# A transformer block on one core: the order of the first feed-forward product on three engines, written out by hand

## The chip, the cores and the metric

The kernel runs on one core of one Trainium2 chip. The metric is the device time of one execution in microseconds (us), from the first to the last instruction with what lies around them; the time of a kernel is the median of its runs.

## What is computed

One block of a hybrid encoder on 512 tokens of width 2048: an input projection, two kinds of attention, an output projection, and a feed-forward part of width 8192. The change touches the first of the two feed-forward products:

```python
h2 = rmsnorm(x, g_mlp[l])
u = jax.nn.relu(jnp.einsum('bsd,df->bsf', h2, w_up[l]))      # the first product
x = x + jnp.einsum('bsf,fd->bsd', u * u, w_down[l])          # the second
return rmsnorm(x, g_final)
```

## The kernel before

Everything is float32 in and out. The matrix engine works in a faster form of float32 with fewer bits, so an operand is split into a high part (a cast on ACT, `split`, line 65) and a low part (the difference, on DVE, line 66), and a product is the sum of high times high and the two cross products.

**The first feed-forward product** is cut into `NU` = 32 units of 256 columns of `w_up`. In each unit the product is a 2 by 2 block product with seven instead of eight multiplications (Winograd's form of Strassen's scheme). The seven are numbered 1 to 7. The activations' seven forms, `F[p]` (high and low, tiles `fh` and `fl`), are made once. The weights of a unit are made into seven parts: blocks 1, 2 and 3 are plain blocks of `w_up`; 5, 6 and 7 are differences of blocks, and 4 is a difference of block 2 and part 6. For most units ("early" ones) the differences for 5, 6 and 7 were made during the attention stage and lie in DRAM (`td`); the others load plain blocks and make them on DVE in the stage itself (`self.raw`, lines 898, 899 and 901).

A unit (`class Unit`) loads three tiles from the pool `rw` of five buffers: `r` (block 1 and part 6), `q` (parts 5 and 7) and a wide one (blocks 2 and 3). `split_part` makes high and low part of one of the seven; `hi_lo` hands out four sets of buffers in turn (three named `wh`/`wl`, one `wx`). `multiply` issues 8 matmuls with the high part over 512 columns (both activation halves, line 920) and 8 with the low part over 256 (line 922). Products 1, 6, 7 and 4 go into one PSUM bank (A, `psa`) and add up there; 2 goes into B, 5 and then 3 into C. Between them `close` takes sums out: after 1, 6 and 7 ACT copies A into a tile `s` (line 933), so the next product into A has to wait for that copy. DVE then adds B or C and writes a quarter of the result `c` (lines 940 to 952). The copies after 1 and 7 share one buffer, so that one must be used up before the next is made. After product 3 the quarter is complete, and ACT applies relu and square (lines 954 and 955).

Two units make a pair, whose result `c` is the input of the second product. It needs seven forms of it in turn, again split into high and low (`store_form`, `hidden_form`): ACT casts into a tile `st` (three buffers), DVE makes the low part in the same tile, and SP stores it to DRAM (`ufd`, line 962).

**What sets the order.** The loop over units (line 1149 on) calls products in the order new 1, old 4, new 5, new 6, old 3, new 2, new 7, with one form stored behind four of them. In this loop no engine's order is written by hand: the framework's scheduler sorts all engines' instructions by its own timing model. Each engine then runs its list strictly in that order, and so does SP, which issues all the DMAs.

Of the kernel before, what the change touches and what calls it, by code (L numbers as in the profile page):

```python
# [40 lines left out]
def block_kernel(ctx, tc, x, g_attn, w_in, b_f, g_out_sb, g_out_fox, w_out, g_mlp, w_up, w_down, g_final, y):  # L41
# [21 lines left out]
    def split(hi, lo, src, scale=None):  # L63
        if scale is None:
            ins = casts[0] = act.copy(hi, src)  # L65
            lows[0] = dve.tensor_tensor(lo, src, hi.bitcast(F32), op=ALU.subtract)  # L66
# [780 lines left out]
    class Unit:  # L847
        def __init__(self, u):
            self.u = u
            first, last = (up_rows[i][:, :, 2 * u * P:2 * (u + 1) * P] for i in range(2))  # L850
# [6 lines left out]
            def blocks():  # L857
                return rw.tile([P, 2, KC // 2, P], F32, tag="rw", name="wu")

            def wide(src):  # L860
                raw = rw.tile([P, KC // 2, 2 * P], F32, tag="rw", name="wu")
                sp.dma_start(raw, src)
                return [raw[:, :, j * P:(j + 1) * P] for j in range(2)]

            r, q = blocks(), blocks()
            b11, t2, t1, t3 = r[:, 0], r[:, 1], q[:, 0], q[:, 1]
            sp.dma_start(b11, first[:, :, :P])
            self.raw = u not in early
            if self.raw:
                sp.dma_start(t1, first[:, :, P:])  # L870
                sp.dma_start(t3, last[:, :, P:])
                sp.dma_start(t2, last[:, :, P:])
            else:
                for t_, j in ((t1, 0), (t2, 2), (t3, 1)):
                    sp.dma_start(t_, td[u][:, j])
            b21, b22 = wide(last)
            self.b = {1: b11, 5: t1, 6: t2, 2: b21, 7: t3, 3: b22, 4: b21}
            self.open_banks()

        def open_banks(self):  # L880
            self.B, self.C, self.A = (ups.tile([P, NT], F32, tag=c, name=f"ps{c}") for c in "bca")
# [11 lines left out]
            self.b.update({3: b22, 4: b21})  # L893

        def split_part(self, p):
            hi, lo = (w.rearrange("p (a b) -> p a b", b=P) for w in hi_lo(2 * NT))
            if p == 5 and self.raw:
                dve.tensor_tensor(self.b[7], self.b[7], self.b[5], op=ALU.subtract)
                dve.tensor_tensor(self.b[5], self.b[5], self.b[1], op=ALU.subtract)
            if p == 6 and self.raw:  # L900
                dve.tensor_tensor(self.b[6], self.b[6], self.b[5], op=ALU.subtract)
            if p == 4 and self.u < 2:
                dve.tensor_tensor(self.b[4], self.b[4], self.b[6], op=ALU.subtract)
            split(hi, lo, self.b[p])
            if p == 2 and self.u > 1:
                dve.tensor_tensor(self.b[4], self.b[4], self.b[6], op=ALU.subtract)
            self.parts[p] = hi, lo

        def product(self, p):
            if p not in self.parts:  # L910
                self.split_part(p)
            self.multiply(p)
            self.close(p)

        def multiply(self, p):
# [5 lines left out]
            for a in range(KC // 2):  # L921
                pe.matmul(ps[:, :2 * P], lo[:, a, :], F[p][a // 4][:, a % 4, 0, :], start=False, stop=a == KC // 2 - 1, skip_group_check=True)  # L922

        def close(self, p):
# [5 lines left out]
            t1, t2 = slice(0, 2 * P), slice(2 * P, NT)  # L930
            if p in (1, 6, 7):
                self.m = (sr if p == 6 else sm).tile([P, NT], F32, tag="m", name=f"s{p}", bufs=2 if p == 6 else 1)
                act.copy(self.m, self.A)
                if p == 6:
                    self.m6 = self.m
                if p == 1:
                    self.m1 = self.m

            def sums(out, m):
                dve.tensor_tensor(out, m[:, t1], m[:, t2], op=ALU.add)  # L940

            if p == 7:
                dve.tensor_tensor(self.m, self.m, self.C, op=ALU.add)
                sums(self.c[:, 1, t2], self.m)
            if p == 2:
                dve.tensor_tensor(self.m1, self.m1, self.B, op=ALU.add)
                sums(self.c[:, 0, t1], self.m1)
            if p == 4:
                act.copy(self.c[:, 0, t2], self.A[:, t1])
                dve.tensor_tensor(self.c[:, 0, t2], self.c[:, 0, t2], self.A[:, t2], op=ALU.add)  # L950
            if p == 3:
                dve.tensor_tensor(self.m6, self.m6, self.C, op=ALU.add)
                sums(self.c[:, 1, t1], self.m6)
                act.activation(self.c, self.c, AF.Relu)
                act.activation(self.c, self.c, AF.Square)

    def store_form(p, c, u):
        st = wp.tile([P, 2, 2, 2 * P], F32R, tag="wraw", name="st")
        hidden_form(p, c, (st[:, 0], st[:, 1]), c[:, :, 1, 2 * P:])
        (g0, j0), (g1, j1) = (at_unit[u + i] for i in range(2))  # L960
        if g0 == g1:
            sp.dma_start(ufd[g0][p][:, :, j0:j0 + 2, :], st.bitcast(F32))
# [185 lines left out]
    old = u1  # L1148
    for u in range(2, NU + 1):
        new = Unit(u) if u < NU else None  # L1150
        if u == NU - 1:
            for p in ORDER:
                load_uf(p, GROUPS[0])
            b_first = load_b(GROUPS[0], 0)
        if new is None:
            second(1, b_first, 0, GROUPS[0][1], True)
        for i, (who, p) in enumerate(((new, 1), (old, 4), (new, 5), (new, 6), (old, 3), (new, 2), (new, 7))):
            if who is None:
                continue
# [1 line left out]
            if u == 3 and p == 6:
                v2 = cp.tile([P, TB], F32, name="v2")
                dve.tensor_reduce(v2, ss2, axis=mybir.AxisListType.X, op=ALU.add)
                dve.tensor_scalar(v2, v2, 1.0 / D, EPS, op0=ALU.mult, op1=ALU.add)
                ev = cp.tile([P, TB], F32, name="ev")
                dve.scalar_tensor_tensor(ev, v2, EPS, v2, op0=ALU.mult, op1=ALU.mult)
            if todo and u < NU - 1 and i in (0, 2, 4, 5):
                store_form(*todo.pop(0))
            if p == 3 and who.u % 2 == 1 and who.u < NU - 2:
                todo += [(q, who.pair, who.u - 1) for q in A_ORDER]  # L1170
# [161 lines left out]
```

## Time and profile before

| | |
|---|---|
| median of 3 runs | 2067.24 us (2059.48 to 2069.8) |
| profiled execution | 2065.28 us, its span 2063.6 us |
| busy PE, DVE, ACT | 99%, 80%, 52% of the span |
| first feed-forward product | about 795 to 1437 us of the span |

PE is the matrix engine, DVE and ACT the two elementwise engines, SP the queue that issues the DMAs. Times in the trace are microseconds from the start of the span. A group's row gives its count, its busy time, the mean of one in ns, and the idle time of its engine just ahead of it with what ended it. A matmul's end in the trace is modelled; its start is measured.

### The profile page before, as it was taken

What the parts mean: (1) busy time and instruction counts of PE and PEld (TensorE: products, weight loads), DVE (VectorE), ACT (ScalarE), POOL (GpSimd) and SP (SyncE); (2) the same over time, 40 slices, a digit from 0 to 9 for tenths busy, and PEclk for the clock granted to TensorE, in tenths of its full rate; (3) what the DMA queues carried; (4) which work ended last, traced back from release to release, by engine and by line L of the source; (5) the groups of instructions that cost most, each with busy time, mean ns of one, the idle gap of its engine ahead of it and who ended that gap; (6) DMA issues with size and microseconds to landing.
All of it is one profiled execution on the core that took longest, in us unless ns stands there. A gap on an engine that the chain in (4) does not pass through costs nothing.

```text
span 2063.6 us, 26764 instructions
## 1 busy us (share of the span) xinstructions
PE 2033.8 (99%) x10188; PEld 1727.3 (84%) x10188; DVE 1656.2 (80%) x1866; ACT 1071.4 (52%) x1419; POOL 59.7 (3%) x73
## 2 busy tenths in 40 slices
PE   8999999999999999999999999999999999999998
PEld 8888888888888888888888888888888888888886
DVE  4767767767777779888888888978889889888886
ACT  5334334444546577656656666655744444443433
POOL 0000000000101000000000000000000000000003
PEclk9999999999999999999999999999999999999999
DMA  7888977888764867777876877777875764764722
GB/s 237 276 289 277 293 256 263 285 268 278 251 200 139 271 226 222 241 258 251 271 240 228 262 246 247 260 249 248 295 247 214 267 243 152 269 234 134 267 91 102
DMA packets 371728, 492.60 MB, mean 239 GB/s; under 512 B 12760, under 2 KB 258568, under 8 KB 362512
## 3 DMA queue, kind: packets, MB, share of 16 engines
q1 hardware_dynamic: 370640, 488.77, 71.5%
q10 hardware_dynamic: 960, 2.13, 0.3%
q8 instruction: 80, 1.31, 0.2%
q14 instruction: 48, 0.39, 0.1%
HBM read 373.39 MB, written 117.46 MB: 238 GB/s over the span
## 4 chain that ended last, share of the span: by engine, by line
PE 91%; DMA 3%; DVE 3%; ACT 2%; issue 1%; SPq 0%; ACTq 0%; DVEq 0%
PE psa L920 10%; PE accd L99 8%; PE accd L100 8%; PE accd L98 8%; PE accq L98 5%; PE accq L99 5%; PE accq L100 5%; PE psa L922 5%; PE psc L920 5%; PE psb L920 3%; PE accv L98 3%; PE accv L99 3%; PE accv L100 3%; PE psc L922 2%; DMA ufd<-st 2%; PE psb L922 1%
## 5 line engine op out<-in xcount | busy, mean ns | idle before, releaser
L65 ACT CAST wh<-wraw 128x1024 fp32r<-128x1024 f32 (+2 forms) x157 | 160.9, 1025 | 241.2 <-PE accq L99 117.3
L66 DVE TENSOR_TENSOR wl<-wraw,wh 128x1024 fp32r<-128x1024 f32 (+2 forms) x157 | 186.5, 1189 | 101.6 <-ACT wh L65 101.1
L65 ACT CAST wh<-wd 128x1024 fp32r<-128x1024 f32 (+1 forms) x134 | 132.6, 999 | 182.0 <-PE accd L100 125.5
L65 ACT CAST wh<-wu 128x1024 fp32r<-128x1024 f32 x160 | 166.9, 1049 | 107.3 <-PE psa L920 39.0
L66 DVE TENSOR_TENSOR wl<-wu,wh 128x1024 fp32r<-128x1024 f32 x160 | 194.9, 1222 | 29.5 <-ACT wh L65 23.9
L98 PE MATMUL accq<-hH,wh 128*128 128x512 f32 x512 | 201.2, 393 | 0.0
L100 PE MATMUL accq<-hH,wl 128*128 128x512 f32 x512 | 199.9, 390 | 0.0
L99 PE MATMUL accq<-hL,wh 128*128 128x512 f32 x512 | 199.7, 390 | 0.0
L66 DVE TENSOR_TENSOR wl<-wd,wh 128x1024 fp32r<-128x1024 f32 (+1 forms) x134 | 153.3, 1155 | 34.2 <-ACT wh L65 34.0
L99 PE MATMUL accd<-wl,uf 128*128 128x512 f32 x428 | 166.8, 390 | 0.4 <-DVE wl L66 0.4
L98 PE MATMUL accd<-wh,uf 128*128 128x512 f32 x428 | 166.6, 390 | 0.1
L100 PE MATMUL accd<-wh,uf 128*128 128x512 f32 x428 | 166.6, 389 | 0.0
L65 ACT CAST wx<-wd 128x1024 fp32r<-128x1024 f32 (+1 forms) x90 | 89.5, 1001 | 118.0 <-PE accd L100 77.4
L66 DVE TENSOR_TENSOR wx<-wd,wx 128x1024 fp32r<-128x1024 f32 (+1 forms) x90 | 103.3, 1158 | 21.9 <-ACT wx L65 21.8
L99 PE MATMUL accd<-wx,uf 128*128 128x512 f32 x292 | 114.0, 390 | 0.5 <-DVE wx L66 0.3
L98 PE MATMUL accd<-wx,uf 128*128 128x512 f32 x292 | 113.6, 390 | 0.2 <-ACT wx L65 0.2
L100 PE MATMUL accd<-wx,uf 128*128 128x512 f32 x292 | 113.7, 389 | 0.0
L100 PEld LDWEIGHTS accq<-hH,wl 128*128 128x128 f32 x512 | 96.1, 188 | 20.1
L99 PEld LDWEIGHTS accq<-hL,wh 128*128 128x128 f32 x512 | 96.2, 188 | 19.0
L98 PEld LDWEIGHTS accq<-hH,wh 128*128 128x128 f32 x512 | 96.2, 188 | 18.8
L1028 DVE TENSOR_TENSOR m<-m,accd 128x1024 f32<-128x1024 f32 x84 | 102.4, 1219 | 11.4 <-PE accd L100 11.3
L920 PE MATMUL psa<-fh,wh 128*128 128x512 f32 x392 | 106.9, 393 | 0.0
(308 smaller groups left out, 4829.8 us busy)
## 6 DMA issues: line engine op xcount, KB each, us to landing
ufd<-st SPq DMA_DIRECT2D x98, 512.0 KB, 6.1
wd<-in_w_down_dram SPq DMA_DIRECT2D x48, 1024.0 KB, 7.3
wraw<-in_w_in_dram SPq DMA_DIRECT2D x84, 512.0 KB, 5.8
uf<-ufd SPq DMA_DIRECT2D x42, 1024.0 KB, 6.4
wu<-in_w_up_dram SPq DMA_DIRECT2D x66, 512.0 KB, 6.9
wu<-in_w_up_dram SPq DMA_DIRECT2D x32, 1024.0 KB, 8.5
sums<-in_w_up_dram SPq DMA_DIRECT2D x60, 512.0 KB, 5.6
td<-sums SPq DMA_DIRECT2D x20, 1536.0 KB, 5.9
```

The costliest lines, as they stand in the source:

```text
L65: ins = casts[0] = act.copy(hi, src)
L66: lows[0] = dve.tensor_tensor(lo, src, hi.bitcast(F32), op=ALU.subtract)
L98: pe.matmul(out, sh, mh, start=first, stop=False, skip_group_check=True)
L99: pe.matmul(out, sh, ml, start=False, stop=False, skip_group_check=True)
L100: pe.matmul(out, sl, mh, start=False, stop=last, skip_group_check=True)
L920: pe.matmul(ps, hi[:, a, :], both, start=a == 0 and p in (1, 2, 5), stop=False, skip_group_check=True)
L922: pe.matmul(ps[:, :2 * P], lo[:, a, :], F[p][a // 4][:, a % 4, 0, :], start=False, stop=a == KC // 2 - 1, skip_group_check=True)
L1028: dve.tensor_tensor(M[p][:, :, db, :], M[p][:, :, db, :], ps, op=ALU.add)
```

## The change

From unit 2 to unit 30 the loop is replaced by a table `SLOTS` with one list of steps for even and one for odd units, which sets the order on ACT and DVE as written (`tc.manual_schedule` for both) and on PE (its manual order now reaches to the end of this loop). A step names what is done and for which unit: `P` a product, `c` a cast, `l` a low part, `m` ACT's copy of bank A, `a` DVE's additions, `rs` one of the three sums of a unit that makes its own weights, `b4` the difference for product 4, `ld` a load, `sq` relu and square, each for `o` (the old unit), `u` (this one) or `n` (the next); `fs`, `fc`, `fl` and `fd` are sum, cast, low part and store of one of the seven forms of an earlier pair. The sum of a form now stands ahead of its cast as a step of its own and may overwrite a quarter of `c`. The units that make their own weights become 3, 7, 9, 11, 13, 15, 17, 19, 23, 25, 27 and 29; they were 2, 5, 7, 10, 13, 15, 18, 21, 23, 26, 29 and 31 (twelve either way). The number of instructions on each engine and of DMAs stays the same; unit 31 and all that follows are ordered by the scheduler as before.

PE, at the end of unit 29 (`psa_12215`) and the start of unit 30 (`psa_12404`, `psc_12403`), before:

```order
L920 MATMUL psa_12215<-fh7_6265,wh_12370 128x512 x4
L920 MATMUL psa_12215<-fl7_6266,wh_12370 128x512 x4
L922 MATMUL psa_12215<-fh7_6265,wl_12371 128x256 x4
L922 MATMUL psa_12215<-fl7_6266,wl_12371 128x256 x4
L922 MATMUL psa_12404<-fl1_6258,wl_12406 128x256
L922 MATMUL psc_12403<-fh5_6542,wl_12455 128x256 x4
L922 MATMUL psc_12403<-fl5_6543,wl_12455 128x256 x4
L920 MATMUL psa_12215<-fh4_6261,wx_12432 128x512 x4
```

The same place now (unit 29 is `psa_12226`, unit 30 `psa_12416` and `psc_12415`):

```order
L931 MATMUL psa_12226<-fh7_6265,wl_12310 128x256 x4
L931 MATMUL psa_12226<-fl7_6266,wl_12310 128x256 x4
L929 MATMUL psa_12416<-fh1_6257,wh_12333 128x512 x4
L929 MATMUL psa_12416<-fl1_6258,wh_12333 128x512 x4
L931 MATMUL psa_12416<-fh1_6257,wl_12334 128x256 x4
L931 MATMUL psa_12416<-fl1_6258,wl_12334 128x256 x4
L929 MATMUL psc_12415<-fh5_6542,wx_12385 128x512 x4
L929 MATMUL psc_12415<-fl5_6543,wx_12385 128x512 x4
L931 MATMUL psc_12415<-fh5_6542,wx_12386 128x256 x4
L931 MATMUL psc_12415<-fl5_6543,wx_12386 128x256 x4
L929 MATMUL psa_12226<-fh4_6261,wh_12389 128x512 x4
```

Unit 30's products 1 and 5 moved as a whole between unit 29's 7 and 4, where before their low halves were split off and only nine short matmuls stood between.

ACT at the same place, before (`s7_12390` is the copy of unit 29's bank after product 7, `st` a form's cast, L954 and L955 are relu and square of unit 28):

```order
L954 ACTIVATE c_12174<-c_12174 128x1024
L65 CAST st_12474<-c_11805 128x512
L955 ACTIVATE c_12174<-c_12174 128x1024
L65 CAST wh_12501<-wu_12211 128x1024
L65 CAST wh_12553<-wu_12395 128x1024
L933 COPY s7_12390<-psa_12215 128x512
```

Now (the copy is `s7_12433`):

```order
L962 ACTIVATE c_12218<-c_12218 128x1024
L963 ACTIVATE c_12218<-c_12218 128x1024
L938 COPY s7_12433<-psa_12226 128x512
L910 CAST wh_12436<-wu_12248 128x1024
L910 CAST wh_12439<-wu_12133 128x1024
L938 COPY s1_12447<-psa_12416 128x512
L910 CAST wx_12467<-wu_12312 128x1024
L978 CAST st_12474<-c_11846 128x512
L978 CAST st_12476<-c_11846 128x512
```

The copy moved ahead of the casts, and the forms' casts behind it.

DVE, where unit 29 makes its own weights, before (L898, L899 and L901 are the three sums, `wu_12206` and `wu_12205` unit 29's tiles):

```order
L898 TENSOR_TENSOR wu_12206<-wu_12206 128x1024
L940 TENSOR_TENSOR c_11805<-s7_12018 128x256
L906 TENSOR_TENSOR wu_12028<-wu_12028,wu_12022 128x8x128
L899 TENSOR_TENSOR wu_12206<-wu_12206,wu_12205 128x1024
L66 TENSOR_TENSOR wl_12182<-wu_12023,wh_12181 128x1024
L950 TENSOR_TENSOR c_11805<-c_11805,psa_11846 128x256
L901 TENSOR_TENSOR wu_12205<-wu_12205,wu_12206 128x1024
L952 TENSOR_TENSOR s6_11940<-s6_11940,psc_11845 128x512
```

Now (L884 are the sums, `wu_12098` and `wu_12072` unit 29's tiles):

```order
L914 TENSOR_TENSOR wx_12168<-wu_12072,wx_12167 128x1024
L943 TENSOR_TENSOR c_11846<-c_11846,psa_11854 128x256
L884 TENSOR_TENSOR wu_12098<-wu_12098 128x1024
L884 TENSOR_TENSOR wu_12098<-wu_12098,wu_12072 128x1024
L951 TENSOR_TENSOR s6_11970<-s6_11970,psc_11853 128x512
L953 TENSOR_TENSOR c_11846<-s6_11970 128x256
L884 TENSOR_TENSOR wu_12072<-wu_12072,wu_12098 128x1024
L914 TENSOR_TENSOR wl_12195<-wu_12098,wh_12194 128x1024
```

The sums moved behind unit 29's first low part and the addition after unit 27's product 4; two stand in a row, and the addition after product 3 is done before the third.

The core of the diff:

```diff
-    early = [u for u in range(NU) if u % 8 not in (2, 5, 7)]
+    early = [u for u in range(NU) if u % 2 == 0 or u in (1, 5, 21, 31)]
...
+        def raw_sum(self, p):
             if self.raw:
...
+                a, b = {7: (7, 5), 5: (5, 1), 6: (6, 5)}[p]
+                dve.tensor_tensor(self.b[p], self.b[a], self.b[b], op=ALU.subtract)
...
+    class Form:
...
+        def add(self):
+            a, b, op = {5: (self.a21, self.a22, ALU.add), 6: (self.a22, self.a11, ALU.subtract),
+                        7: (self.a11, self.a21, ALU.subtract), 3: (self.a12, self.a22, ALU.subtract)}[self.p]
+            dve.tensor_tensor(self.src, a, b, op=op)
+
+        def high(self):
+            self.st = wp.tile([P, 2, 2, 2 * P], F32R, tag="wraw", name="st")
+            act.copy(self.st[:, 0], self.src)
...
-    for who, p in ((u0, 6), (u1, 5), (u0, 7), (u1, 6), (u0, 4), (u1, 7), (u0, 3)):
+    SLOTS = [("P u 1; m o 7; fs 6; c u 6; c o 3; a o 7; ld n r; m u 1; P u 5; l u 6; l o 3; c u 2; ld n q; "
...
+             ("P u 1; fc 0; fl 0; fc 1; ld n r; m o 7; c u 6; a o 7; P u 5; c o 3; l u 6; l o 3; fd 0; fl 1; "
...
+    rows_cm = tc.manual_schedule(engines={act.engine, dve.engine})
+    rows_cm.__enter__()
...
+    for u in range(2, NU - 1):
+        units_[u + 1] = Unit(u + 1)
+        at = {"o": units_[u - 1], "u": units_[u], "n": units_[u + 1]}
+        first_of = u - 3 - (u + 1) % 2
+        at["u"].open_banks()
+        for step in SLOTS[u % 2].split(";"):
...
+    rows_cm.__exit__(None, None, None)
     out_cm.__exit__(None, None, None)
...
-        for i, (who, p) in enumerate(((new, 1), (old, 4), (new, 5), (new, 6), (old, 3), (new, 2), (new, 7))):
+        for i, (who, p) in enumerate(((new, 1), (new, 5), (old, 4), (new, 6), (old, 3), (new, 2), (new, 7))):
```

More of the change, by code (lines that the diff above doesn't have):

```diff
@@ L855, in __init__ @@
                 return
[L857 to L867, printed above, removed]
@@ L868, in __init__ @@
-            self.raw = u not in early
-            if self.raw:
[L870 to L878, printed above, removed]
+            self.raw = u not in early
@@ new lines, in __init__, with load_r, load_q @@
+            self.b, self.c = {}, None
+        def load_r(self):
+            self.r = rw.tile([P, 2, KC // 2, P], F32, tag="rw", name="wu")
+            u = self.u
+            sp.dma_start(self.r[:, 0], up_rows[0][:, :, 2 * u * P:(2 * u + 1) * P])
+            sp.dma_start(self.r[:, 1], up_rows[1][:, :, (2 * u + 1) * P:2 * (u + 1) * P] if self.raw else td[u][:, 2])
+            self.b.update({1: self.r[:, 0], 6: self.r[:, 1]})
+        def load_q(self):
+            q = rw.tile([P, 2, KC // 2, P], F32, tag="rw", name="wu")
+            u = self.u
+            for j in range(2):
+                sp.dma_start(q[:, j], up_rows[j][:, :, (2 * u + 1) * P:2 * (u + 1) * P] if self.raw else td[u][:, j])
+            self.b.update({5: q[:, 0], 7: q[:, 1]})
@@ new lines, in load_wide @@
+        def load_wide(self):
+            raw = rw.tile([P, KC // 2, 2 * P], F32, tag="rw", name="wu")
+            u = self.u
+            sp.dma_start(raw, up_rows[1][:, :, 2 * u * P:2 * (u + 1) * P])
+            b21, b22 = (raw[:, :, j * P:(j + 1) * P] for j in range(2))
+            self.b.update({2: b21, 3: b22, 4: b21})
+        def raw_sum(self, p):
+            if self.raw:
+                a, b = {7: (7, 5), 5: (5, 1), 6: (6, 5)}[p]
+                dve.tensor_tensor(self.b[p], self.b[a], self.b[b], op=ALU.subtract)
@@ L895, in split_part, with high, low @@
         def split_part(self, p):
[L896 to L907, printed above, removed]
+            self.high(p)
+            self.low(p)
+        def high(self, p):
+            self.parts[p] = [w.rearrange("p (a b) -> p a b", b=P) for w in hi_lo(2 * NT)]
+            casts[0] = act.copy(self.parts[p][0], self.b[p])
+        def low(self, p):
+            hi, lo = self.parts[p]
+            lows[0] = dve.tensor_tensor(lo, self.b[p], hi.bitcast(F32), op=ALU.subtract)
         def product(self, p):
@@ L913, in product @@
             self.close(p)
+            if p == 3:
+                self.square()
         def multiply(self, p):
@@ L922, in multiply, with copy_sum, add_sum @@
                 pe.matmul(ps[:, :2 * P], lo[:, a, :], F[p][a // 4][:, a % 4, 0, :], start=False, stop=a == KC // 2 - 1, skip_group_check=True)
-        def close(self, p):
+        def copy_sum(self, p):
+            if p == 4:
+                act.copy(self.c[:, 0, 2 * P:], self.A[:, :2 * P])
+                return
+            self.m[p] = (sr if p == 6 else sm).tile([P, NT], F32, tag="m", name=f"s{p}", bufs=2 if p == 6 else 1)
+            act.copy(self.m[p], self.A)
+        def add_sum(self, p):
+            t1, t2 = slice(0, 2 * P), slice(2 * P, NT)
+            if p == 4:
+                dve.tensor_tensor(self.c[:, 0, t2], self.c[:, 0, t2], self.A[:, t2], op=ALU.add)
+                return
             if p == 2:
@@ L929, in close @@
                 self.c = hidden[0][:, self.u % 2]
[L930 to L955, printed above, removed]
+            m = self.m[{7: 7, 2: 1, 3: 6}[p]]
@@ new lines, in add_sum, with close, square @@
+            dve.tensor_tensor(m, m, self.B if p == 2 else self.C, op=ALU.add)
+            out = {7: self.c[:, 1, t2], 2: self.c[:, 0, t1], 3: self.c[:, 1, t1]}[p]
+            dve.tensor_tensor(out, m[:, t1], m[:, t2], op=ALU.add)
+        def close(self, p):
+            if p in (1, 6, 7, 4):
+                self.copy_sum(p)
+            if p in (7, 2, 3, 4):
+                self.add_sum(p)
+        def square(self):
+            act.activation(self.c, self.c, AF.Relu)
+            act.activation(self.c, self.c, AF.Square)
@@ new lines, in block_kernel, with __init__, low, store @@
+    class Form:
+        def __init__(self, i, c, u):
+            self.p, self.u = A_ORDER[i], u
+            self.a11, self.a21, self.a12, self.a22 = (c[:, :, i, j:j + 2 * P] for i in range(2) for j in (0, 2 * P))
+            self.src = {1: self.a11, 2: self.a12, 5: self.a22, 6: self.a22, 4: self.a22, 7: self.a21, 3: self.a12}[self.p]
+        def add(self):
[5 more added lines that the diff above has]
+            act.copy(self.st[:, 0], self.src)
+        def low(self):
+            dve.tensor_tensor(self.st[:, 1], self.src, self.st[:, 0].bitcast(F32), op=ALU.subtract)
+        def store(self):
+            put_form(self.p, self.st, self.u)
@@ L1143, in block_kernel, with store_next @@
     u1.others()
-    for who, p in ((u0, 6), (u1, 5), (u0, 7), (u1, 6), (u0, 4), (u1, 7), (u0, 3)):
-        who.product(p)
-    more_parts.append(parts_hx)
+    def store_next(k=1):
+        for _ in range(k):
+            if todo:
+                store_form(*todo.pop(0))
+    SLOTS = [("P u 1; m o 7; fs 6; c u 6; c o 3; a o 7; ld n r; m u 1; P u 5; l u 6; l o 3; c u 2; ld n q; "
[7 rows of a table added]
+    units_ = {0: u0, 1: u1}
+    units_[2] = Unit(2)
+    u2 = units_[2]
+    for who, p in ((u0, 6), (u1, 5), (u0, 7), (u1, 6)):
+        who.product(p)
@@ new lines, in block_kernel @@
+    u2.load_r()
+    u0.last_sum()
+    u0.product(4)
+    u2.load_q()
+    u2.load_wide()
+    u1.product(7)
+    more_parts.append(parts_hx)
+    rows_cm = tc.manual_schedule(engines={act.engine, dve.engine})
+    rows_cm.__enter__()
+    u0.split_part(3)
+    u2.split_part(1)
+    u2.split_part(5)
+    u1.last_sum()
+    u0.multiply(3)
+    u1.split_part(4)
+    u0.close(3)
+    u0.square()
+    forms = {}
+    for u in range(2, NU - 1):
[4 more added lines that the diff above has]
+        for step in SLOTS[u % 2].split(";"):
+            what, who, *p = step.split()
+            if what[0] == "f":
+                if first_of < 0:
+                    continue
+                i = int(who)
+                if (first_of, i) not in forms:
+                    forms[first_of, i] = Form(i, units_[first_of].pair, first_of)
+                getattr(forms[first_of, i], {"fs": "add", "fc": "high", "fl": "low", "fd": "store"}[what])()
+                continue
+            who, p = at[who], (int(p[0]) if p and p[0].isdigit() else p)
+            if u == 2 and who is u1 and p == 7:
+                continue
+            if what == "ld":
+                getattr(who, {"r": "load_r", "q": "load_q", "w": "load_wide"}[p[0]])()
+            elif what == "b4":
+                who.last_sum()
+            elif what == "sq":
+                who.square()
+            else:
+                getattr(who, {"P": "multiply", "c": "high", "l": "low", "m": "copy_sum", "a": "add_sum", "rs": "raw_sum"}[what])(p)
+        if u == 3:
+            v2 = cp.tile([P, TB], F32, name="v2")
+            dve.tensor_reduce(v2, ss2, axis=mybir.AxisListType.X, op=ALU.add)
+            dve.tensor_scalar(v2, v2, 1.0 / D, EPS, op0=ALU.mult, op1=ALU.add)
+            ev = cp.tile([P, TB], F32, name="ev")
+            dve.scalar_tensor_tensor(ev, v2, EPS, v2, op0=ALU.mult, op1=ALU.mult)
@@ L1147, in block_kernel @@
+    todo += [(q, units_[NU - 4].pair, NU - 4) for q in A_ORDER]
+    rows_cm.__exit__(None, None, None)
     out_cm.__exit__(None, None, None)
-    old = u1
-    for u in range(2, NU + 1):
-        new = Unit(u) if u < NU else None
+    old = units_[NU - 2]
+    for u in range(NU - 1, NU + 1):
+        new = units_.get(u)
         if u == NU - 1:
+            new.open_banks()
             for p in ORDER:
@@ L1154, in block_kernel @@
             b_first = load_b(GROUPS[0], 0)
+            old.close(7)
         if new is None:
             second(1, b_first, 0, GROUPS[0][1], True)
-        for i, (who, p) in enumerate(((new, 1), (old, 4), (new, 5), (new, 6), (old, 3), (new, 2), (new, 7))):
+        for i, (who, p) in enumerate(((new, 1), (new, 5), (old, 4), (new, 6), (old, 3), (new, 2), (new, 7))):
             if who is None:
@@ L1160, in block_kernel @@
             who.product(p)
[L1161 to L1170, printed above, removed]
+            if who is new and p == 2:
+                new.last_sum()
         old = new
```

6 lines of the change are left out of this document (5 added, 1 removed), and 6 rows, old and new, of the table SLOTS.

## The prediction

> **What bounds the kernel now.** I read the page first, then PE's own waits, then the timeline around the longest of them. Two lines: the page's busy row, and the windows row of the first feed-forward product.
>
> ```profile
> PE 2033.8 (99%) x10188; PEld 1727.3 (84%) x10188; DVE 1656.2 (80%) x1866; ACT 1071.4 (52%) x1419; POOL 59.7 (3%) x73
> 830.00:1437.00 607.00, 596.96 (x3396) 524.16 (x3395) 519.81 (x649) 383.45 (x496) 0.00 (x0) 1.00 0.76 250
> ```
>
> PE is the bound; the change adds and removes no matmul. Inside the stage PE is idle for 607.00 - 596.96 = 10.0 us, so this is about the gain on offer. PE's list of waits (us, times, longest) names who ends the idle time:
>
> ```profile
> PE psa L920 <- ACT s L933: 8.5, 7, 2.7
> PE psc L920 <- ACT wh L65: 1.5, 1, 1.5
> ```
>
> The longest of the seven, on three engines' timelines (start, us, what):
>
> ```profile
> 1389.42 1.09 PE L920 MATMUL psa<-fh,wh 128*128 128x512 f32 x4
> 1392.33 0.64 PE L922 MATMUL psc<-fh,wl 128*128 128x256 f32 x4
> 1392.81 0.64 PE L922 MATMUL psc<-fl,wl 128*128 128x256 f32 x4
> 1396.12 1.21 PE L920 MATMUL psa<-fh,wx 128*128 128x512 f32 x4 [2.67 <-ACT s L933]
> 1397.16 1.09 PE L920 MATMUL psa<-fl,wx 128*128 128x512 f32 x4
> ...
> 1387.97 1.05 ACT L954 ACTIVATE c<-c 128x1024 f32<-128x1024 f32 x1
> 1392.12 0.62 ACT L65 CAST st<-c 128x512 fp32r<-128x512 f32 x1 [3.10 <-DMA ufd<-st]
> 1392.65 1.05 ACT L955 ACTIVATE c<-c 128x1024 f32<-128x1024 f32 x1
> 1393.61 1.98 ACT L65 CAST wh<-wu 128x1024 fp32r<-128x1024 f32 x2
> 1395.49 0.57 ACT L933 COPY s<-psa 128x512 f32<-128x512 f32 x1
> ...
> 1383.01 11.00 SPq L962 DMA_DIRECT2D ufd<-st  x4
> ```
>
> Product 7 of the old unit starts at 1389.42 and, at 2.79 us a product (below), ends at 1392.21. Product 4 of that unit accumulates into the same bank and must wait until ACT has copied the bank out. Only nine short matmuls stand between them, 1.08 us. ACT has the copy fifth in its order: it sat 3.10 us before a form's cast, whose tile a store still held, then did a square and two casts for later products. The copy starts at 1395.49 instead of about 1392.5.
>
> **The change part by part.** *The stalls that go.* The waits list gives 8.5 + 1.5 = 10.0 us of idle. By starts each costs more: the last psc group starts at 1392.81, its four take 0.48 (1392.33 to 1392.81 is such a group), so 1396.12 - 1393.29 = 2.83, which is 0.16 over the 2.67 shown; the first group after it takes 1397.16 - 1396.12 = 1.04 against 0.93 in an undisturbed product (below), another 0.11. Eight stalls: 8 x 0.27 = 2.2. After the one at 1073 the granted clock fell:
>
> ```profile
> 1074.40:1078.00 3.60, 3.60 (x15) 3.17 (x14) 1.18 (x3) 1.31 (x2) 0.00 (x0) 0.53 0.99 297
> ```
>
> 3.60 x (1 - 0.53) = 1.7 us. Together 10.0 + 2.2 + 1.7 = 13.9 us, if all go. [...]
>
> *The new order.* PE's rows now run u1, u5, o4, u6, o3, u2, u7 (u this unit, o the one before), each whole. A product's period:
>
> ```profile
> 1012.10 1.09 PE L920 MATMUL psa<-fh,wh 128*128 128x512 f32 x4
> 1013.03 1.07 PE L920 MATMUL psa<-fl,wh 128*128 128x512 f32 x4
> 1013.94 0.64 PE L922 MATMUL psa<-fh,wl 128*128 128x256 f32 x4
> 1014.89 1.09 PE L920 MATMUL psc<-fh,wh 128*128 128x512 f32 x4
> ```
>
> 2.79 us, its low half from 1.84. With u1 at 0 the others start at 2.79, 5.58, 8.37, 11.16, 13.95, 16.74, and the next unit at 19.53. So o4 follows o7 after two products, 5.58 us, not 1.08. Durations for ACT and DVE, groups of the stretch 880 to 1400:
>
> ```profile
> L66 DVE TENSOR_TENSOR wl<-wu,wh 128x1024 fp32r<-128x1024 f32 x136 | 165.6, 1222 | 23.0 <-ACT wh L65 18.1 <-PE psa L922 2.3 <-issue 1.8
> L66 DVE TENSOR_TENSOR st<-c,st 128x512 fp32r<-128x512 f32 x91 | 60.6, 688 | 19.8 <-ACT st L65 19.7
> L940 DVE TENSOR_TENSOR c<-s 128x256 f32<-128x256 f32 x78 | 32.8, 421 | 0.3
> L943 DVE TENSOR_TENSOR s<-s,psc 128x512 f32<-128x512 f32 x26 | 17.7, 683 | 0.8 <-ACT s L933 0.8
> L898 DVE TENSOR_TENSOR wu<-wu 128x1024 f32<-128x1024 f32 x10 | 12.2, 1224 | 7.1 <-DMA wu<-in_w_up_dram 7.1
> L950 DVE TENSOR_TENSOR c<-c,psa 128x256 f32<-128x256 f32 x25 | 10.4, 415 | 0.0
> L65 ACT CAST wh<-wu 128x1024 fp32r<-128x1024 f32 x136 | 141.8, 1049 | 87.8 <-PE psa L920 29.3 <-PE psc L920 16.9 <-DVE wl L66 12.1
> L65 ACT CAST st<-c 128x512 fp32r<-128x512 f32 x91 | 53.5, 619 | 40.2 <-DMA ufd<-st 39.8
> L933 ACT COPY s<-psa 128x512 f32<-128x512 f32 x78 | 45.2, 579 | 11.2 <-DVE c L940 7.9 <-PE psa L922 3.3
> L955 ACT ACTIVATE c<-c 128x1024 f32<-128x1024 f32 x26 | 27.5, 1058 | 0.3
> L949 ACT COPY c<-psa 128x256 f32<-128x256 f32 x26 | 9.7, 371 | 0.7 <-PE psa L922 0.7
> ```
>
> I laid the rows of an even and an odd slot after one another with these, every cast waiting for the high half of the product four before it. ACT's work per pair of units: 14 x 1.05 + 6 x 0.58 + 2 x 0.37 + 4 x 1.06 + 7 x 0.62 = 27.5 us of 39.1. DVE's, with the three raw sums: 14 x 1.22 + 5 x 1.22 + 6 x (0.68 + 0.42) + 2 x 0.42 + 11 x 0.69 = 38.2 of 39.1; without them 34.6. The even slot with raw sums: o7's bank copied by 1.0, DVE's low of u6 done at 3.2 and of o3 at 5.3, the raw sums start at 14.2, o3's addition ends at 17.7, the squares at 20.8, the low of u4 at 22.5. The odd slot starts with DVE 3.0 and ACT 1.3 late: two form casts, o7's copy until 3.2 (o4 needs it by 5.58), u6, o3 and u2 cast by 6.3, u1's bank copied by 6.9 (u6 needs it by 8.37), low of u7 at 13.6 (needed at 18.6), of u4 at 21.3. It returns DVE 1.8 late, and the next even slot ends at 22.5 again. So nothing holds PE, and the tightest places are u1's copy in odd slots (1.4 us) and o7's (2.4 us). The forms' sums ahead of their casts and the weights' sums three rows earlier than their casts cost nothing: they are the same instructions in DVE's slack, which is gone where DVE is over 2.8 us later than this.
>
> *The transfers.* SP's loads keep their places: q behind o3's low, the wide load behind the sum for product 4. What SP is moved past are the stores.
>
> ```profile
> ufd<-st SPq DMA_DIRECT2D x84, 512.0 KB, 5.9
> wu<-in_w_up_dram SPq DMA_DIRECT2D x55, 512.0 KB, 6.7
> DMA to landing us min/median/max: 3.6/6.5/11.0
> DMA to landing us min/median/max: 2.5/5.7/10.7
> ```
>
> (The last two: loads into wu, stores from st.) In an odd slot form 1 is stored at about 8 and form 4's cast at 14.0 needs its tile: at 5.9 us it fits, at 10.7 ACT waits 4.7 us, of which the copy of o7 in the next slot bears 4.2; PE would lose 0.5 + 0.27 = 0.8. In an even slot with raw sums q is issued at 6.1 and 6.5; at 6.7 it lands at 13.2, before 14.2; at 11.0 the sums are 3.3 us late, 2.3 of it borne, and PE loses 1.0 + 0.27 = 1.3. Bounds: 0, and 14 pairs x 0.8 + 12 raw units x 1.3 = 27 us; a gain is excluded, since all of PE's idle time in the stage is already in the 13.9. The medians are the commonest landings, so I take the lower end for both.
>
> *Odd weight sums, the ends.* Twelve units sum their own weights before and after; they now lie in odd units alone, at most one in a pair, as before. The start (units 2 and 3) and the end (unit 31, where the scheduler takes over, and one form of 0.62 + 0.69 us more falls into the second product, beside its work) aren't in the walk. I leave one stall of the mean size there, 10.0 / 8 + 0.27 = 1.5 us; from 0 to 3.
>
> Sum: 13.9 - 1.5 = 12.4 us. The profiled execution's 2065.28 becomes 2052.9. The median of the runs shown, 2067.24, is 1.96 above that execution, so 2054.8.
>
> **The rivals.** *A: the slack isn't there.* Loads and stores land late often enough that PE stalls again, at half the bounds' mean: 7 us of the 13.9 come back. For it: ACT's 39.8 us before form casts, and landings up to 11.0. Against: the waits on raw loads were 7.1 us in seven, and are borne up to 2.3 each. 2067.24 - 13.9 + 1.5 + 7 = 2061.8.
>
> *B, the other side: DVE becomes the bound.* From unit 7 to 19 every odd unit sums its own weights, seven pairs in a row, where before every fourth pair had none. A raw stretch of before:
>
> ```profile
> 1273.00:1313.00 40.00, 39.98 (x231) 35.03 (x229) 35.60 (x45) 26.49 (x36) 0.00 (x0) 1.00 0.77 253
> ```
>
> DVE is busy for about 35.6 us of 39.1, so its order may hold 3.5 us of waits in a pair. In the stage it waited 607.00 - 519.81 = 87.2 us, 5.6 in each of 15.5 pairs. Should a fixed order keep 5.6, a raw pair takes 41.2 and 12 of them cost 25 us, against 13.9 gained: 2067.24 + 11 = 2078. It decides from 3.5 + 13.9 / 12 = 4.7 us a pair. Against it: many of those waits are DVE ahead of its work, and the walk has about 1 us of them.
>
> **How the numbers follow.** 0.5% of 2067.24 is 10.3 us, about what a measurement of this kernel can tell from no change: 2056.9. The forecast (one to three stalls left) has 0.58, A 0.33, B 0.09; so faster 0.58, same 0.33, slower 0.09. The range goes from all 13.9 us gone and half the spread of the three runs (2059.48 to 2069.8, so 5.2) below that, 2048, to A with nearly the whole gain lost, 2066. The forecast's own range is 2050 to 2057.
>
> **What would show it.** Right: PE's waits on ACT's copy of psa under 2 us in total, the window of the stage 12 us shorter at the same PE busy time, product 4 two products behind 7 with no idle, ACT's wait on stores well under 39.8. Wrong: PE waiting for the copy of u1's bank in odd slots, or for a low part; DVE over 37 us busy per pair in units 6 to 19 with PE idle beside it; SP holding stores behind a load. If the stretch behind the stage (1437 to the end) took another time than before, the sum would be wrong at a place that it doesn't look at.

## The result and the profile after

The median went from 2065.11 us (7 runs, 2059.48 to 2069.80) to 2053.72 us (7 runs, 2052.75 to 2056.38). The ratio is 0.9949, its 95% interval 0.9934 to 0.9964: 10.5 us less by the ratio (11.4 by the medians), just over the half per cent that the prediction sets as the bound between faster and the same, with an interval that reaches to both sides of it. The profiled execution took 2052.75 us, the shortest of the seven; its span of 2051.0 us is 12.6 below the one before. Of the four runs of experiment `x2` below, one of 3405.73 us at a granted clock of 0.556 is left out of the median.

The busy row of the page, and the windows row of the part that is ordered by hand (from, to, length, then each engine's busy time, the granted clock, the DMA share, GB/s):

```profile
PE 2029.8 (99%) x10188; PEld 1724.9 (84%) x10188; DVE 1666.0 (81%) x1866; ACT 1077.9 (53%) x1419; POOL 59.7 (3%) x73
830.00:1427.00 597.00, 596.32 (x3409) 524.07 (x3408) 531.20 (x654) 390.93 (x499) 0.00 (x0) 1.00 0.78 253
```

PE is now idle for 597.00 - 596.32 = 0.7 us there, where 10.0 stood before. The stage's length is read from its first matmul to the first one of the second product, on PE's timeline. Before:

```profile
795.28 1.07 PE L920 MATMUL psa<-fh,wh 128*128 128x512 f32 x4
...
1439.73 0.50 PE L98 MATMUL accd<-wx,uf 128*128 128x512 f32 x1 [0.19 <-ACT wx L65]
```

After:

```profile
794.26 1.07 PE L929 MATMUL psa<-fh,wh 128*128 128x512 f32 x4
...
1425.92 0.49 PE L98 MATMUL accd<-wx,uf 128*128 128x512 f32 x1 [0.19 <-ACT wx L65]
```

644.45 us became 631.66, so the stage gave 12.8. It began 1.0 earlier, and what follows it takes 625.1 instead of 623.9, 1.2 longer; 12.8 + 1.0 - 1.2 = 12.6, the whole difference of the spans. The waits of PE in the stage (us, times, longest), all that are left:

```profile
PE psc L929 <- DVE s L951: 0.4, 1, 0.4
PE accd L98 <- ACT wx L65: 0.2, 1, 0.2
```

The seven waits for ACT's copy and the one for a cast are gone; what is left at 830 is a new one, 0.4 us. ACT's own waits on the forms' stores and on the weights' sums, 880 to 1437:

```profile
ACT st L978 <- DMA ufd<-st: 13.4, 11, 1.6
ACT wh L910 <- DVE wu L884: 46.7, 11, 4.3
```

The first fell from 39.8 (longest 6.7); the second is long, and nothing on PE hangs on it. The odd slot, which the prediction called the tightest, on PE and ACT:

```profile
1239.92 1.09 PE L929 MATMUL psa<-fh,wh 128*128 128x512 f32 x4
1242.72 1.09 PE L929 MATMUL psc<-fh,wh 128*128 128x512 f32 x4
1245.51 1.09 PE L929 MATMUL psa<-fh,wx 128*128 128x512 f32 x4
...
1248.30 1.09 PE L929 MATMUL psa<-fh,wh 128*128 128x512 f32 x4
...
1240.72 1.14 ACT L978 CAST st<-c 128x512 fp32r<-128x512 f32 x2
1241.77 0.58 ACT L938 COPY s<-psa 128x512 f32<-128x512 f32 x1
1242.25 1.99 ACT L910 CAST wh<-wu 128x1024 fp32r<-128x1024 f32 x2
1244.76 1.06 ACT L910 CAST wh<-wu 128x1024 fp32r<-128x1024 f32 x1 [0.51 <-PE psc L929]
1245.71 0.58 ACT L938 COPY s<-psa 128x512 f32<-128x512 f32 x1
```

The old unit's product 7 ends at 1239.92, where the new unit's product 1 starts. The copy of its bank ends at 1242.35, so it is 2.43 us late, and product 4 starts at 1245.51, 5.59 after the end of 7. I call the first number the *lateness* and the second, as far as PE's own work fills it, the *distance*; PE stands still where lateness exceeds distance. In even slots the lateness is 0.79. The new unit's product 1 ends at 1242.72, the copy of its bank at 1246.29, and product 6, which needs that bank, starts at 1248.30: 2.0 us to spare. Behind no copy of a bank into `s` is less left in units 4 to 29.

### The profile page after: what moved, and what is told of

It reads as the page before. It is cut to its first block, busy times and chain, and to the rows that moved or that the text cites. A ratio compares the mean times of both kernels' runs of the same rounds, so it can differ in the third digit from the quotient of the medians.

```text
span 2051.0 us, 26668 instructions
## 1 busy us (share of the span) xinstructions
PE 2029.8 (99%) x10188; PEld 1724.9 (84%) x10188; DVE 1666.0 (81%) x1866; ACT 1077.9 (53%) x1419; POOL 59.7 (3%) x73
## 3 DMA queue, kind: packets, MB, share of 16 engines
q10 hardware_dynamic: 960, 2.13, 0.3%
## 4 chain that ended last, share of the span: by engine, by line
PE 92%; DVE 3%; DMA 2%; ACT 1%; issue 1%; SPq 1%; ACTq 0%; DVEq 0%
PE psa L929 11%; PE accd L99 7%; PE accd L98 7%; PE accd L100 7%; PE psa L931 6%; PE psc L929 5%; PE accq L98 5%; PE accq L100 5%; PE accq L99 5%; PE psc L931 3%; PE psb L929 3%; PE accv L98 3%; PE accv L99 3%; PE accv L100 3%; PE psb L931 1%; PE acca L100 1%
```

## The experiments

Four things can be set apart: the list of units that make their own weights, PE's order by hand, ACT's and DVE's order by hand (never one of these two alone), and the place of single steps in it. All ratios are against the kernel before, run on the same chip.

**1 and 2. One half of the hand's order at a time.** In `x1` ACT and DVE go back to the scheduler, in `x2` PE does; the rest is the changed kernel.

```diff
 # x1
-    rows_cm = tc.manual_schedule(engines={act.engine, dve.engine})
+    rows_cm = ExitStack()
 # x2
+    out_cm.__exit__(None, None, None)      # PE's manual order ends ahead of the loop
     rows_cm = tc.manual_schedule(engines={act.engine, dve.engine})
```

> The changed kernel with PE's order as written, but ACT and DVE left to the scheduler in units 2 to 30. Theory 1 (PE's order did it: product 4 now follows product 7 after 5.55 us of other products, where it was 0.96 to 5.55 before): ACT's copies may come as late as before (up to 7.1 us after product 7's end), but only two or three of the seven stalls are longer than the new distance; PE's idle time in the stage is 1 to 3 us, the gain against the kernel before 9 to 12 us. Theory 2 (ACT's and DVE's order did it: the copy ahead of the forms' casts): the stalls stay, PE's idle time is 6 to 10 us and the gain under 5 us.

> The changed kernel with ACT's and DVE's orders as written, but PE left to the scheduler from unit 2 on; it puts 4.59 or 5.55 us of other products between 7 and 4, and 1.92 to 5.55 us between 6 and 7. Theory 1 (PE's order did it): with 1.92 us between 6 and 7 PE stalls there, in every second of some twenty units; 5 to 10 us of idle. Theory 2 (ACT's order did it): the copies come 1.6 to 3.6 us after a product's end as in the changed kernel, so most distances suffice, and where it is 1.92 a copy that takes 1.62 fits; idle under 3 us and the gain of 10 to 13 us is kept.

x1: 2053.57 us, ratio 0.9953 (0.9938 to 0.9968). x2: 2052.88, 0.9948 (0.9932 to 0.9965). Both are as fast as the whole change. The windows rows of the stage, x1 and then x2:

```profile
830.00:1427.00 597.00, 596.54 (x3410) 524.37 (x3409) 518.92 (x651) 385.73 (x495) 0.00 (x0) 1.00 0.77 253
```

```profile
830.00:1427.00 597.00, 596.72 (x3415) 525.17 (x3414) 530.52 (x656) 389.01 (x499) 0.00 (x0) 1.00 0.78 254
```

Theory 1 missed for x2, and theory 2 for x1. In x1 the copies end up to 5.54 us after product 7, but the distance is 5.59 everywhere (one wait of 0.3 is left, product 6's for a copy). The latest of them, on PE and ACT:

```profile
1182.08 1.09 PE L929 MATMUL psa<-fh,wh 128*128 128x512 f32 x4
...
1187.67 1.20 PE L929 MATMUL psa<-fh,wh 128*128 128x512 f32 x4
...
1187.04 0.58 ACT L938 COPY s<-psa 128x512 f32<-128x512 f32 x1
```

Product 7 ends at 1182.08, the copy at 1187.62, and product 4 starts at 1187.67. In x2 the scheduler leaves 4.6 or 5.6 us between 7 and 4, but the copy is at most 3.2 late; the latest:

```profile
1161.76 1.09 PE L929 MATMUL psa<-fh,wh 128*128 128x512 f32 x4
...
1167.35 1.09 PE L929 MATMUL psa<-fh,wx 128*128 128x512 f32 x4
...
1164.34 0.58 ACT L938 COPY s<-psa 128x512 f32<-128x512 f32 x1
```

Here either side of the comparison is enough. ACT's wait for stores need not fall for it: in x1 it is still 30.0 us.

**3. The copy's early place under a short distance.** `e2` exchanges products 5 and 4, and with them their casts and low parts, so that only one product stands between 7 and 4; all three engines stay by hand.

```diff
-m u 1; P u 5; l u 6; ...   fl 5; P o 4; fl 6; ...   c n 5; P u 7; ...
+m u 1; P o 4; l u 6; ...   fl 5; P u 5; fl 6; ...   c u 4; P u 7; ...
```

> The changed kernel with products 4 and 5 exchanged on PE (u1, o4, u5, u6, o3, u2, u7), and their casts and low parts with them: product 4 follows 7 after 2.78 us again. By the changed kernel's trace the copy after 7 ends 0.8 us after product 7's end in even slots and 2.42 in odd ones, so 0.3 us are left. Theory 1 (the distance did it): ACT is later than that somewhere in most pairs, 14 odd slots lose 0.3 to 1 us each; idle 4 to 12 us. Theory 2 (the copy's place on ACT did it): idle under 3 us, the time within 3 us of the changed kernel.

2053.31 us, 0.9950 (0.9935 to 0.9965); the distance is 2.79 in every slot, the lateness 0.8 to 1.3. In odd slots ACT's relu and square, which stand ahead of the copy, start 2.5 us before product 7 ends and not 1.4 as in the changed kernel, so the copy is sooner done.

```profile
830.00:1427.00 597.00, 596.72 (x3411) 524.54 (x3410) 531.46 (x654) 392.08 (x498) 0.00 (x0) 1.00 0.78 253
```

Theory 1 missed: I had carried over the changed kernel's lateness of 2.42, which leaves 0.3 us, and expected ACT to be later than that in most pairs. With the copy this early, one product between 7 and 4 is enough; the 1.08 us that stood there ahead of the longest stall before would not always have been.

**4. Nothing by hand.** `x3` keeps the list and the steps as they are written, but the scheduler orders all three engines.

> The changed kernel with no order written by hand in units 2 to 30: the table's steps, the loads in three pieces and the new list of own-weight units stay, but the scheduler sorts PE, ACT and DVE. Theory A (a stall is the copy's lateness minus the distance that PE's order leaves; before, up to 6.8 us against 0.96 to 6.85; either half written by hand lifts one of the two): without both, distances of 1.87 to 3.7 us are back for a dozen units, lateness is near the 5.5 us of the run with PE alone by hand, so PE idles 4 to 10 us in the stage and the gain falls to 2 to 8 us. Theory C (the new list and the steps' new sequence did it, the writing by hand nothing): idle under 1 us, the gain of 10 to 12 us stays.

2062.42 us, 0.9982 (0.9970 to 0.9994). PE's waits in the stage:

```profile
PE psa L929 <- ACT s L938: 6.1, 5, 2.2
```

Stalls of the old kind return, five of them, at other units. The order on the engines makes the gain, as theory A has it.

**5, 6 and 7. From the kernel before upwards: the list, PE's order, and both.** `y1` takes the new list alone, `y3` PE's order alone (by hand, with new 5 ahead of old 4), `y4` the two; ACT and DVE stay with the scheduler.

```diff
 # y1, y4
-    early = [u for u in range(NU) if u % 8 not in (2, 5, 7)]
+    early = [u for u in range(NU) if u % 2 == 0 or u in (1, 5, 21, 31)]
 # y3, y4: out_cm, PE's manual order, ends ahead of unit 31, and
-        for i, (who, p) in enumerate(((new, 1), (old, 4), (new, 5), (new, 6), (old, 3), (new, 2), (new, 7))):
+        for i, (who, p) in enumerate(((new, 1), (new, 5), (old, 4), (new, 6), (old, 3), (new, 2), (new, 7))):
```

> The kernel before with the new list of own-weight units alone. Theory A: the list changes neither how late ACT is (held by the forms' stores, not by DVE) nor the distances much (1.92 to 5.55 us), so PE idles 6 to 12 us in the stage and the time stays within 4 us of before. Theory C: much of the gain, 6 us or more, comes from the list.

> The kernel before with PE's order alone written by hand in the new sequence (new 1, new 5, old 4, new 6, old 3, new 2, new 7), units 2 to 30; the list, the loads and the forms as before. Theory A: copies after product 7 come up to 6.8 us late as before, the distance is 5.59 everywhere, so of the seven stalls two remain, 0.3 and 1.2 us, and perhaps the one of a late cast (1.5 us); idle 1 to 4 us, gain 9 to 13 us. Theory C: the stalls stay with the old list and forms, idle 6 us or more, gain under 5 us.

> The kernel before, with the new list of units that make their own weights and with PE's order by hand (new 1, new 5, old 4, ...); ACT and DVE stay with the scheduler, forms as before. With PE's order alone 5.4 us of stalls were left, in three places, units 9, 17 and 25, each one ahead of an even unit that made its own weights (10, 18, 26); the list alone was worth about 1 us. Theory 1 (the two parts need each other: the list takes these three places away): no stall over 0.3 us in the stage's steady part, 2053 to 2055. Theory 2 (what is missing is the hand's placing of forms' sums and casts on ACT and DVE): the copy after product 7 is still over 5.6 us late in some units, 3 to 6 us of stalls stay, 2057 to 2060.

y1: 2063.58 us, 0.9990 (0.9980 to 1.0001), not told from no change; six stalls on the copy, in other units than before:

```profile
PE psa L920 <- ACT s L933: 7.9, 6, 2.6
```

y3: 2059.20 us, 0.9969 (0.9958 to 0.9979), about six tenths of the gain, less than I expected. Stalls on the copy are left at units 9, 17 and 25 only, two at each; the first pair, on PE and ACT:

```profile
993.45 1.19 PE L920 MATMUL psa<-fh,wh 128*128 128x512 f32 x4 [0.30 <-ACT s L933]
...
997.46 0.74 PE L920 MATMUL psa<-fh,wh 128*128 128x512 f32 x2 [0.95 <-ACT s L933]
...
989.44 0.62 ACT L65 CAST st<-c 128x512 fp32r<-128x512 f32 x1 [3.60 <-DMA ufd<-st]
989.97 2.00 ACT L65 CAST wh<-wu 128x1024 fp32r<-128x1024 f32 x2
991.87 1.05 ACT L954 ACTIVATE c<-c 128x1024 f32<-128x1024 f32 x1
992.83 0.57 ACT L933 COPY s<-psa 128x512 f32<-128x512 f32 x1
```

Product 7 ended at 987.39. A form's cast waited 3.60 us, by this row for a store, and two casts and a relu stand between it and the copy: lateness 6.0, over the 5.59 that PE's order gives. At unit 17 the cast at the same place waited 3.66 us, and the trace names one of the sums that unit 18 makes of its own weights; each of the three units is followed by an even one that makes them. Which of the two, the store or the sums, holds the cast was not separated.

y4: 2052.31 us, 0.9945 (0.9931 to 0.9959), theory 1.

```profile
830.00:1427.00 597.00, 596.81 (x3413) 524.68 (x3411) 520.64 (x652) 386.40 (x498) 0.00 (x0) 1.00 0.77 255
```

Two edits on the kernel before, a line for the list and PE's order, bring the whole gain; its interval overlaps that of the full change, so neither is shown faster. It has little in hand, though. Unit 29 in y4, PE and ACT:

```profile
1377.51 1.09 PE L920 MATMUL psa<-fh,wh 128*128 128x512 f32 x4
...
1383.09 1.09 PE L920 MATMUL psa<-fh,wh 128*128 128x512 f32 x4
...
1381.76 0.62 ACT L65 CAST st<-c 128x512 fp32r<-128x512 f32 x1 [2.26 <-DMA ufd<-st]
1382.28 0.58 ACT L933 COPY s<-psa 128x512 f32<-128x512 f32 x1
```

Product 7 ends at 1377.51, the copy at 1382.86, product 4 starts at 1383.09: 0.2 us to spare, and as little once behind a copy after product 1. In the changed kernel the smallest margin behind product 7 is 5.59 - 2.43 = 3.2, and 2.0 behind any copy.

**8 and 9. The list under the hand's order.** `e1` takes the old list back into the changed kernel, with the sums as steps in odd slots too; `e1b` is the same with unit 3 in the place of unit 2.

```diff
-    early = [u for u in range(NU) if u % 2 == 0 or u in (1, 5, 21, 31)]
+    early = [u for u in range(NU) if u % 8 not in (2, 5, 7)]                          # e1
+    early = [u for u in range(NU) if u == 2 or u % 8 not in (2, 5, 7) and u != 3]     # e1b
...
-l n 1; fc 4; fd 2; P o 3; a o 3; fl 3; P u 2;
+l n 1; rs n 7; fc 4; fd 2; P o 3; rs n 5; a o 3; fl 3; P u 2; rs n 6;
 # and, ahead of the loop
+    for p in (7, 5, 6):
+        u2.raw_sum(p)
     u2.split_part(5)
```

> The changed kernel with the old list of units that make their own weights (2, 5, 7, 10, 13 and so on), the three sums written into the odd slots' list too, between the low part of the next unit's block 1 and the squares. Main theory (DVE's slack holds them: 35.8 us of 39.1 in a pair with sums): the sums delay DVE by 3.7 us in slots 9, 17 and 25, o7's addition in the slot behind ends at about 7.3 and u1's copy at 7.9, needed at 8.37; idle 0 to 2 us in the stage, the time within 3 us of the changed kernel. Rival (the odd list was needed, since odd slots hold five of the seven forms): more than 1 us of PE idle in each of the slots 10, 18 and 26 and 4 to 10 us in all.

> The changed kernel with the old list of units that make their own weights, but with unit 3 in the place of unit 2 (3, 5, 7, 10, 13, 15, 18, 21, 23, 26, 29, 31), and the sums as steps in odd slots too. With unit 2 in the list 8.5 us were lost in one stall where the stage's order by hand begins. Theory 1 (that stall at the start is all that the old list costs, the slots hold sums in either): no PE idle over 0.3 us in units 4 to 30, 2053 to 2055. Theory 2 (sums in odd slots delay product 4's weights or the copy of unit 1's product a little each time): stalls of 0.5 to 1 us ahead of units 10, 18 and 26, 2055 to 2058.

e1: 2062.01 us, 0.9985 (0.9975 to 0.9994). Nearly all of the loss lies in one place, where the order by hand begins (behind it, from 844 to 1427, PE has no idle time); PE's timeline and the windows row behind the stall:

```profile
838.69 2.04 PE L929 MATMUL psc<-fh,wx 128*128 128x512 f32 x4 [5.75 <-DVE s L951]
840.53 1.91 PE L929 MATMUL psc<-fl,wx 128*128 128x512 f32 x4
...
838.69:844.00 5.31, 5.31 (x17) 4.54 (x18) 2.17 (x3) 4.93 (x6) 0.00 (x0) 0.50 0.00 0
```

Unit 2's three sums, as I placed them, stand on DVE ahead of the addition that empties bank C for product 5, and the first of them waits 1.91 us for its load. The stall of 5.75 us and a clock of 0.50 for the 5.3 us behind it make 5.75 + 2.7 = 8.4 us, and e1 lacks 2062.01 - 2053.72 = 8.3 (0.4 of the stall stands in the changed kernel too). Neither theory has this place: the main one allowed 3 us in all, and the rival looked for stalls in slots 10, 18 and 26, where none came. e1b: 2054.39 us, 0.9953 (0.9941 to 0.9966), theory 1, and its row shows 0.6 us of idle:

```profile
830.00:1427.00 597.00, 596.44 (x3408) 523.77 (x3406) 530.05 (x654) 389.30 (x497) 0.00 (x0) 1.00 0.78 253
```

So under the hand's order the slots hold sums in even units as well, and what the list does there is to keep unit 2 out. Under the scheduler (y3 against y4) it was worth three pairs of stalls on the copy.

**10. The forms' sums.** `e5` moves two of the forms' sums (6 and 2) back to stand directly ahead of their own casts. (The expectation says three; two were moved.)

```diff
-m o 7; fs 6; c u 6; ... fc 5; fc 6; ...   fs 2; ld n q; ... ld n w; fc 2; ...
+m o 7; c u 6; ... fc 5; fs 6; fc 6; ...   ld n q; ... ld n w; fs 2; fc 2; ...
```

> The changed kernel with three of the forms' sums (6, 2 and the like) moved back to stand directly ahead of their own casts; nothing else. Theory 1 (DVE and ACT have slack for it; the sums' place costs and brings nothing): within 1 us of the changed kernel, 2053 to 2054.5, PE idle under 0.5 us in the stage's steady part. Theory 2 (each cast then waits for a sum that stands behind other work on DVE, and the copies behind the cast are late): 0.5 to 1 us a pair, 2059 to 2067.

2054.42 us, 0.9953 (0.9941 to 0.9966), theory 1: the lateness of the copies after products 7 and 1 as in the changed kernel, and PE idle for 0.4 us of the stage. For these two forms the early sum brings and costs nothing that shows.

**11 and 12. How much DVE can take.** The low part of the next unit's product 1 is made three times (`e4_two_more_lows`) or twice (`e4_one_more_low`) in every slot, into the same tile.

```diff
-l n 1; a o 4; ...    l n 1; fc 4;
+l n 1; l n 1; a o 4; ...    l n 1; l n 1; fc 4;      # one more; a third "l n 1" for two more
```

> The changed kernel with the low part of the next unit's block 1 made three times in each slot instead of once (the same values written again): 2 x 1.14 us more for DVE per unit, 4.6 per pair. It tests how far off the rival of the prediction was in which DVE becomes the bound. By the changed kernel's trace DVE is busy for 35.8 of 39.1 us in a pair with own weights and 32.7 in one without: 40.4 and 37.3 now. If DVE's waits can all be squeezed out, the twelve pairs with own weights take 1.3 us more each, 15 us in all; with the 1 us of waits that the walk through the rows had, 2.3 each, 27 us. If DVE is not in PE's way at all (the low parts' lead of up to three products takes it up), nothing.

> The changed kernel with the low part of the next unit's product 1 made twice in every slot (2.28 us more on DVE a pair, the same result written again). DVE is then busy for 38.1 us in a pair with sums, of PE's 39.1. With two more, a pair with sums took 41.50 us at 40.33 us of DVE, so 1.17 us of waits remained. Theory 1 (about 1.2 us a pair are all the waits that DVE's order needs): a pair with sums takes 39.1 to 39.3, the whole 0 to 3 us more than the changed kernel, 2054 to 2057. Theory 2 (the 3.3 us that DVE waits in such a pair now belong to the order and stay): 41.4 us a pair, twelve pairs, 25 us or more, about 2079.

Two more: 2078.64 us, 1.0062 (1.0047 to 1.0078), 24.9 above the changed kernel, where 15 to 27 was expected if DVE was in PE's way. One more: 2054.40 us, 0.9954 (0.9941 to 0.9967), theory 1. A pair with own sums in the changed kernel, then with one more, then with two more:

```profile
1220.37:1259.46 39.09, 39.09 (x226) 34.40 (x225) 35.79 (x45) 25.85 (x33) 0.00 (x0) 1.00 0.75 242
```

```profile
968.18:1007.27 39.09, 39.09 (x225) 34.40 (x224) 37.96 (x47) 25.83 (x34) 0.00 (x0) 1.00 0.78 256
```

```profile
1014.50:1056.00 41.50, 39.91 (x225) 34.48 (x225) 40.33 (x49) 25.28 (x34) 0.00 (x0) 1.00 0.76 241
```

DVE waits 3.3 us a pair, then 1.1, then 1.2 with the pair stretched to 41.50. Some 1.2 us are all that its order needs with the work added at this place; the rest was DVE ahead of its work. The time is flat up to 38.0 us of DVE in 39.1, and at 40.3 it has grown. PE shows the new bound as the old wait:

```profile
PE psa L929 <- ACT s L938: 16.5, 23, 1.3
```

ACT's copy stands behind casts that wait for DVE; in a stretched pair the copy ends 7.29 us after product 7, and product 4, which PE's order would have at 5.59, starts at 7.33.

## Why the prediction was right, and where it wasn't

The profiled execution was forecast at 2052.9 and took 2052.75; the median was forecast at 2054.8 and came out at 2053.72. The mechanism held, but that the figures meet so closely is partly luck: the profiled execution is the shortest of its seven runs, and the forecast of the median started from 2067.24, where seven runs of the kernel before give 2065.11. Against the forecast fall of 12.4 us stand 12.6 between the spans, 11.4 between the medians and 10.5 by the ratio.

- *The stalls that go, 13.9.* The sum holds: the windows rows lose 10.0 - 0.7 = 9.3 us of idle time, and the other 3.5 of the stage's 12.8 compare with the 3.9 forecast for restarts and the slow clock. The 1.5 left for the start and the end was a little too much, since 13.9 - 12.8 = 1.1 did not come: the start kept one stall (0.4 by the waits list, of the kind that the walk left out, unit 2's product 5 behind DVE's addition), the end none over 0.2. Outside the stage +1.0 and -1.2 cancel by chance.
- *The new order.* The tight places are where the walk put them, with more room: o7's copy in the odd slot ends 2.4 us into the slot (walk: 3.2), u1's copy 6.4 (6.9), the sums in the even slot start at 13.7 (14.2). So the two tightest margins are 3.2 and 2.0 us, not 2.4 and 1.4. The term that was mis-sized is DVE's load, 38.2 us a pair by the walk, 35.8 measured. The 44 instructions of the pair at 1220.37 do add up to 38.2, but neighbours overlap in the trace: two low parts of 1.22 take 2.35 together, as ACT's two casts of 1.05 take 1.99 in the slot shown above:

```profile
1243.63 2.35 DVE L914 TENSOR_TENSOR wl<-wu,wh 128x1024 fp32r<-128x1024 f32 x2
```

  So the sum of these durations put the load 2.4 us too high on DVE, and 1.7 on ACT (27.5 by the walk, 25.85 measured in the same pair).
- *The attribution was too narrow.* I spoke of PE's new rows and ACT's early copy as one cure. Runs 1 to 3 show two cures of which each is enough here: a distance of 5.59 under copies up to 5.54 late, or copies at most 1.3 late under a distance of 2.79.
- *The list "costs nothing".* True of the changed kernel as a whole, but it isn't idle: y3 and y4 differ by it alone, by 6.9 us of the medians or 5.0 of the ratios, and in e1 unit 2 at the start costs 8.4. On the kernel before, by itself, it brings nothing that can be told from no change (y1).
- *The transfers, 0 of up to 27.* The lower end was right: ACT's wait on stores is 13.4 us, at most 1.6 at a time.
- *Rival A* (7 us of stalls come back) was refuted by the waits list. *Rival B* had the right mechanism and the wrong size: a fixed order doesn't keep 5.6 us of waits, it keeps 1.2, so DVE could take another 2.2 us a pair and PE did not stop.
- *The slow clock, 1.7.* It went with the stalls: in no stretch of 2 us between 780 and 1460 does the changed kernel show a granted clock under 1.00, where before 1074 to 1076 showed 0.61 and 1076 to 1078 showed 0.53. The last section has what the traces show of the other drops.

Not tried: ACT's and DVE's order by hand with the old list and PE by the scheduler, and ACT's or DVE's alone.

## What to carry to other kernels

Where an in-order engine must empty a buffer that the bound engine wants back, compare two numbers per use: how late the emptying ends, and how much other work the bound engine's order places in between. Raise the second or lower the first; one is often enough, and doing both buys margin and not time. An engine's idle time in a fixed order can mean that it is ahead, as most of DVE's did here; how much of it the order needs is learnt by giving it more work until the bound engine stops.
